# First-layer convolution taps tied behind score maxima, low weight parts formed by accumulating DMAs, probabilities transposed in row halves

## Chip, cores and metric

The kernel runs on one core of a Trainium2 chip. The metric is the device time of one execution in microseconds (us); the figure for a kernel is the median over its runs. Engines are named as the profile names them: PE is the matrix engine (PEld its weight loads), DVE the vector engine, ACT the scalar engine, POOL the GpSimd engine, SP the engine whose queue issues the loads.

## What is computed

Two layers over 256 latent tokens and 256 context tokens, width 1024. The first sub-layer of each layer has one input projection whose columns feed a convolution branch, an attention and two gates; the second is a gated MLP. Cut to the first sub-layer:

```python
h = modulate(rmsnorm(x, norm1_g[l]), sh1, sc1)
p = h @ w_in[l]                                   # GLU 1024 | q,k,v 3*512 | gates 2*1024
u = a * sigmoid(g)                                # a, g: the two halves of the GLU columns
u = dwconv1d(u, dw, dw_b)                         # 31 taps per channel, 512 channels
u = silu(layernorm(u, ln_g, ln_b));  y_conv = u @ w_conv_out
q, k = rope(q), rope(k)
y_attn = softmax(q k^T + window bias, all context keys) v @ w_na_out
x = x + g1 * ((sigmoid(gc) * y_conv + sigmoid(ga) * y_attn) @ w_out)
...
x = x + g2 * conv_ffn(modulate(rmsnorm(x, norm2_g[l]), sh2, sc2))
```

The context stream goes through the same weights in the first layer only; in the second layer it gives keys and values alone.

## The kernel before

**Weights.** All weights arrive as units of 128 x 1024 float32 (512 KB), in the order in which they are used, through four `raw` buffers that SP fills. `wunit` (L170, work in `wparts`, L150 to L168) splits a unit in two parts: ACT casts it to `whi` (L160, float32r), DVE subtracts to get `wlo = raw - whi` (L161). Four `whi` and four `wlo` buffers rotate. Every product is three matmuls (`mm3`, L178 to L181): `whi` with the high part of the activations, `whi` with the low part, `wlo` with the high part. `unit8` (L193) returns the eight 128-column blocks of a unit. A first-layer unit over both streams (512 columns) is 24 matmuls.

**Units of the input projection.** `U_IN` to `U_IN + 29` are the six remaining GLU units, four q, four k and sixteen gate units. In the first layer the order is q and k of pair 0, two GLU units, q and k of pair 1, two GLU units and so on (`qk`, L749; `glu_groups`, L617), then gates (`gate`, L624).

**Convolution.** `glu` (L602) writes a padded tile `u`; each of the 31 taps is one DVE instruction over 512 columns (L589, L591) that accumulates in `cb`. In the first layer there are two `u` tiles for four channel blocks. Taps wait in a list and are emitted by `conv_run` (L595), `rate[0]` of them (2 in the first layer, 3 in the second) at each `slot()`. A slot comes twice in a 512-column group (L183 to L191) and gives each side generator one step.

**Attention.** `Attention.step` (L416) is a side generator too. With `products` (L442) it issues the scores of two heads (one pair of head halves on rows 0 to 63 and 64 to 127 of the array, L440), with `scores` (L451) the maxima on DVE (L458), exponentials (L461) and normalization (L464) on ACT; `ctx_scores` (L468 to L484) does it for context queries. A later step calls `turn` (L486), which transposes the probabilities (16 PE transposes of 128 x 128: L494 for latent and L499 for context queries) through four PSUM banks, and copies each bank to a `pT` tile on ACT (L495, L500). The step after that calls `values` (L504), whose matmuls (L512) need `pT`. There are four latent and two context steps in the first layer, four latent steps in the second.

**Layer norm of the convolution.** `layer_norm` (L832) emits the taps that are left, adds the four `cb` blocks (two adds on POOL, L842 and L843, one on DVE, L844), and sums over channels on PE (L847).

**Order.** Instructions stand on each engine in the order in which the builder places them; within an engine they start in order. `tc.issue_after(x)` keeps what is issued under it behind instruction `x` in that order.

Of the kernel before, what the change touches and what calls it, by code (L numbers as in the profile page):

```python
# [45 lines left out]
def trunk(ctx: ExitStack, tc: tile.TileContext, xt, cvec, crow, wall, wada, params, bias_t, rope_t, out):  # L46
# [136 lines left out]
    def group(ps, ws, xh, xl, c):  # L183
# [201 lines left out]
    class Attention:  # L385

        def __init__(self, l, eb, T, V, oh, ol):
            self.l, self.eb, self.T, self.V, self.oh, self.ol = l, eb, T, V, oh, ol  # L390
            self.todo, self.soft, self.pv, self.n, self.at = [], [], [], 0, 0
            self.ctx, self.pairs, self.last = [], 0, None

# [22 lines left out]
        def step(self, now=False):  # L416
            self.n += 1
            since = self.n - self.at
            if not now and (since < (4 if self.todo else 3 if self.soft else 2) or not self.todo and self.pairs < 4):
                return  # L420
            if self.todo and not now and self.n - self.todo[0][0] < 2:
                return
            self.at = self.n
            pv, self.pv = self.pv, []
            soft, self.soft = self.soft, []
            for what, its, pps in soft:
                with tc.issue_after(self.last.ins), tc.issue_after(self.done.ins):
# [3 lines left out]
            if self.todo:  # L431
                _, what, its = self.todo.pop(0)
                outs = [self.products(it, [psum(t) for t in tags]) for it, tags in zip(its, (("sc", "sc"), ("pt", "main")))]
                self.soft.append((what, its, [(self.scores if what == LAT else self.ctx_scores)(it, o) for it, o in zip(its, outs)]))

# [15 lines left out]
        def scores(self, it, out):  # L451
            qt, bt = it[1], it[-1]
            pps = []
            for i, ps in enumerate(out):

                mx = small([P, 1], "mx")
                p2, b2 = ps.rearrange("p (a k) -> p a k", a=2), bt[:, 2 * qt + i :: 4 - 2 * qt - i, :]
                dve.tensor_tensor_reduce(p2, p2, b2, -1.0, 3.0e38, ALU.add, ALU.min, mx)  # L458
                pp = self.eb.tile([P, 512], F32, tag="pp", bufs=4, name=nm("pp"))
                sm = small([P, 1], "sm")  # L460
                self.exp = act.activation(pp, ps, AF.Exp, bias=mx, scale=-1.0, accum_out=sm)  # L461
                ri = small([P, 1], "ri")
                dve.reciprocal(ri, sm)
                self.done = act.mul(pp, pp, ri)  # L464
                pps.append(pp)
            return pps

        def ctx_scores(self, it, out):  # L468
            pps = []
            for ps in out:  # L470
                mx = small([P, 2], "mx2")
                dve.tensor_reduce(mx, ps.rearrange("p (q k) -> p q k", q=2), AX.X, ALU.max, negate=True)
                pp = self.eb.tile([P, 512], F32, tag="pp", bufs=4, name=nm("pp"))
# [12 lines left out]
        def turn(self, what, its, pps):  # L486

            pts = [self.eb.tile([P, 4, S], F32, tag="pT", bufs=4, name=nm("pT")) for _ in range(2)]
            for n, tags in enumerate((("sc", "sc"), ("pt", "main"))):
                for i, pp in enumerate(pps[n]):  # L490
                    pt = psum(tags[i])
                    if what == LAT:
                        for kt in range(4):
                            pe.transpose(sl(pt, kt), sl(pp, kt), ident)  # L494
                        act.copy(pts[i][:, :, n * P : (n + 1) * P], pt.rearrange("p (k q) -> p k q", k=4))  # L495
                    else:
                        for t in range(2):
                            for kt in range(2):
                                pe.transpose(pt[:, kt * S + t * P : kt * S + (t + 1) * P], sl(pp, 2 * t + kt), ident)  # L499
                        act.copy(pts[i][:, 2 * n : 2 * n + 2, :], pt.rearrange("p (k q) -> p k q", k=2))  # L500
            js = [its[0][0]] if what == LAT else [it[0] for it in its]
            self.pv.append((what, js, pts))

        def values(self, what, js, pts, bank):  # L504
            po = psum(bank)
            kts = range(4) if what == LAT else range(2, 4)
            for n, j in enumerate(js):
                c = slice(n * S, (n + 1) * S)
                for kt in kts:
                    for i in range(2):  # L510
                        h = 2 * j + i
                        pe.matmul(  # L512
                            po[i * HD : (i + 1) * HD, c], self.V[kt][:, h * HD : (h + 1) * HD],
                            pts[i][:, 2 * n + kt - kts[0], :], start=kt == kts[0], stop=kt == kts[-1],
                        )
# [42 lines left out]
    for l in range(DEPTH):  # L558
# [5 lines left out]
        with ExitStack() if last else start as e1a:  # L564
# [17 lines left out]

            taps = []

            def conv_tap(j, t):
                w = par[:, l * NPAR + DW + j * TAPS + t : l * NPAR + DW + j * TAPS + t + 1]
                src = us[j % NU_][:, :, t : t + S]
                if t == 0:
                    dve.tensor_scalar(cb[j], src, w, pr(l, DWB + j, 1), ALU.mult, ALU.add)  # L589
                else:  # L590
                    dve.scalar_tensor_tensor(cb[j], src, w, cb[j], ALU.mult, ALU.add)  # L591

            rate = [0]

            def conv_run():  # L595
                while True:
                    for _ in range(rate[0]):
                        if taps:
                            conv_tap(*taps.pop(0))
# [33 lines left out]
            with ExitStack() as e1b:  # L633
                eb = e1b.enter_context(tc.tile_pool(name=f"eb{l}", bufs=1))
                V = [eb.tile([P, CONV], F32, name=f"V{l}_{t}") for t in range(4)]
                att = Attention(l, eb, T, V, oh, ol)

# [107 lines left out]
                conv = conv_run()  # L745
                rate[0] = 3 if last else 2
                add_side(conv)
# [68 lines left out]
            with ExitStack() as e1c:  # L816
# [15 lines left out]
                def layer_norm():  # L832
# [392 lines left out]
```

## Time and profile before

| | us |
|---|---|
| three runs | 1127.99, 1128.18, 1128.67 (median 1128.18) |
| the profiled execution | 1127.64 |
| its span, first to last instruction | 1125.9 |
| PE busy | 1114.1 |
| DVE busy | 908.3 |
| ACT busy | 563.6 |
| POOL busy | 14.7 |

A row of the profile names the source line, engine, operation and tiles as `output<-inputs`; of a matmul the moving operand stands first and the stationary one second. `64*128 64x256` says 64 rows of the array, 128 columns, and a moving operand of 64 x 256. Durations of matmuls overlap, since they are pipelined, so the time that one takes from PE is read from the distance between starts.

### The profile page before, as it was taken

What the parts mean: (1) busy time and instruction counts of PE and PEld (TensorE: products, weight loads), DVE (VectorE), ACT (ScalarE), POOL (GpSimd) and SP (SyncE); (2) the same over time, 40 slices, a digit from 0 to 9 for tenths busy, and PEclk for the clock granted to TensorE, in tenths of its full rate; (3) what the DMA queues carried; (4) which work ended last, traced back from release to release, by engine and by line L of the source; (5) the groups of instructions that cost most, each with busy time, mean ns of one, the idle gap of its engine ahead of it and who ended that gap; (6) DMA issues with size and microseconds to landing.
All of it is one profiled execution on the core that took longest, in us unless ns stands there. A gap on an engine that the chain in (4) does not pass through costs nothing.

```text
span 1125.9 us, 17731 instructions
## 1 busy us (share of the span) xinstructions
PE 1114.1 (99%) x6828; PEld 963.0 (86%) x6828; DVE 908.3 (81%) x1631; ACT 563.6 (50%) x934; POOL 14.7 (1%) x24
## 2 busy tenths in 40 slices
PE   9999999999999999999999999999999999999997
PEld 7778777787789988888888888989888999999997
DVE  5689999685778788888898555789996898988773
ACT  4347657542333543434343222544677667766642
POOL 0000000000000000000000000000000000000000
PEclk9999999999999999999999999999999999999999
DMA  9833231536734354554556665556433575565781
GB/s 364 282 94 103 75 118 38 206 97 214 245 118 138 114 161 150 168 169 149 168 171 215 219 191 186 180 181 187 145 126 121 167 250 163 188 194 181 219 268 58
DMA packets 53941, 190.83 MB, mean 169 GB/s; under 512 B 6240, under 2 KB 6496, under 8 KB 53856
## 3 DMA queue, kind: packets, MB, share of 16 engines
q1 hardware_dynamic: 53568, 189.65, 52.1%
q8 instruction: 54, 0.88, 0.3%
q14 instruction: 31, 0.25, 0.1%
q10 hardware_dynamic: 288, 0.04, 0.0%
HBM read 188.62 MB, written 1.05 MB: 168 GB/s over the span
## 4 chain that ended last, share of the span: by engine, by line
PE 83%; DVE 9%; issue 6%; ACT 2%; DMA 0%; POOL 0%; POOLq 0%; DVEq 0%; SPq 0%; ACTq 0%
PE main L179 24%; PE main L181 24%; PE main L180 24%; DVE cb L591 4%; PE main L644 4%; DVE wlo L161 1%; PE sc L181 1%; PE sc L179 1%; PE sc L180 1%; PE po L202 1%; PE po L512 1%; PE sc L129 1%; PE sc L440 0%; DMA sb<-in_crow 0%; PE sc L494 0%
## 5 line engine op out<-in xcount | busy, mean ns | idle before, releaser
L179 PE MATMUL main<-h,whi 128*128 128x256 f32 (+1 forms) x1328 | 446.7, 337 | 0.0
L181 PE MATMUL main<-h,wlo 128*128 128x256 f32 (+1 forms) x1328 | 442.9, 335 | 1.0 <-DVE wlo L161 1.0
L180 PE MATMUL main<-h,whi 128*128 128x256 f32 (+1 forms) x1328 | 442.2, 334 | 0.1
L160 ACT CAST whi<-raw 128x1024 fp32r<-128x1024 f32 (+1 forms) x244 | 252.3, 1039 | 285.5 <-PE main L180 131.5
L161 DVE TENSOR_TENSOR wlo<-raw,whi 128x1024 fp32r<-128x1024 f32 (+1 forms) x244 | 292.9, 1207 | 112.5 <-ACT whi L160 108.0
L179 PEld LDWEIGHTS main<-h,whi 128*128 128x128 f32 x1328 | 249.4, 188 | 32.1 <-issue 3.6
L181 PEld LDWEIGHTS main<-h,wlo 128*128 128x128 f32 x1328 | 249.3, 188 | 29.6 <-DVE wlo L161 1.5
L180 PEld LDWEIGHTS main<-h,whi 128*128 128x128 f32 x1328 | 249.8, 188 | 28.5 <-DVE h L367 0.5
L591 DVE SCALAR_TENSOR_TENSOR cb<-u,par,cb 128x512 f32<-128x512 f32 (+1 forms) x240 | 140.4, 609 | 1.4
L271 DVE CUSTOM_DVE_ANT_0 t<-raw,sb,par 128x1024 bf16<-128x1024 f32 x100 | 126.7, 1277 | 1.0 <-ACT sb L255 0.7
L179 PE MATMUL main<-fh,whi 128*128 128x256 f32 (+1 forms) x386 | 123.0, 319 | 0.0
L180 PE MATMUL main<-fl,whi 128*128 128x256 f32 (+1 forms) x386 | 122.9, 319 | 0.0
L181 PE MATMUL main<-fh,wlo 128*128 128x256 f32 (+1 forms) x386 | 122.9, 318 | 0.0
L180 PEld LDWEIGHTS main<-fl,whi 128*128 128x128 f32 x386 | 72.7, 188 | 5.6
L179 PEld LDWEIGHTS main<-fh,whi 128*128 128x128 f32 x386 | 72.7, 188 | 5.6
L181 PEld LDWEIGHTS main<-fh,wlo 128*128 128x128 f32 x386 | 72.7, 188 | 5.5
L963 ACT ACTIVATE t<-main,par 128x512 f32<-128x512 f32 (+1 forms) x82 | 50.6, 667 | 39.0 <-PE main L181 39.0
L964 DVE SCALAR_TENSOR_TENSOR t<-main,par,t 128x510 f32<-128x510 f32 (+1 forms) x82 | 47.5, 615 | 10.2 <-ACT t L963 9.8
L967 DVE SCALAR_TENSOR_TENSOR t<-main,par,t 128x510 f32<-128x510 f32 (+1 forms) x82 | 46.6, 609 | 0.0
L366 ACT ACTIVATE h<-t,mod 128x256 fp32r<-128x256 f32 x56 | 25.4, 502 | 36.1 <-DVE t L365 36.1
L898 DVE SCALAR_TENSOR_TENSOR x<-main,mod,x 128x256 f32<-128x256 f32 x48 | 22.1, 479 | 23.5 <-PE main L181 23.3
L644 PE MATMUL main<-whi,h 128*128 128x512 f32 x128 | 40.6, 402 | 0.1
(221 smaller groups left out, 1188.2 us busy)
## 6 DMA issues: line engine op xcount, KB each, us to landing
raw<-in_wall SPq DMA_DIRECT2D x239, 512.0 KB, 4.2
raw<-in_wada SPq DMA_DIRECT2D x88, 512.0 KB, 4.3
bias<-in_bias_t SPq DMA_DIRECT2D x8, 640.0 KB, 4.8
row<-in_wada SPq DMA_DIRECT2D x8, 512.0 KB, 4.7
sb<-in_crow SPq DMA_DIRECT2D x5, 512.0 KB, 6.0
x<-in_xt SPq DMA_DIRECT2D x8, 256.0 KB, 4.4
raw<-in_wall SPq DMA_DIRECT2D x8, 256.0 KB, 7.1
out<-t SPq DMA_DIRECT2D x3, 256.0 KB, 2.1
```

The costliest lines, as they stand in the source:

```text
L160: act.copy(hi[:, c], r[:, c])
L161: dve.tensor_tensor(lo[:, c], r[:, c], hi[:, c].bitcast(F32), ALU.subtract)
L179: pe.matmul(ps, w[0], xh, start=start, stop=False)
L180: pe.matmul(ps, w[0], xl, start=False, stop=False)
L181: pe.matmul(ps, w[1], xh, start=False, stop=stop)
L271: dve.tensor_tensor_reduce(tmp().bitcast(BF16), r, v, 1.0, pr(l, BADA + n, 1), ALU.mult, ALU.add, mods[l][:, n, s : s + 1])
L366: high = act.activation(hi[:, c], y[:, c], AF.Identity, bias=b)
L591: dve.scalar_tensor_tensor(cb[j], src, w, cb[j], ALU.mult, ALU.add)
L644: mm = pe.matmul(pv[t], h1[n == 1][k][:, c], w[n == 2][:, b], start=k + n == 0, stop=k == KD - 1 and n == 2)
L963: act.activation(c, pv_, AF.Identity, bias=pr(l, FDB + t, 1), scale=w[1])
L964: dve.scalar_tensor_tensor(c[:, :, 1:], pv_[:, :, : S - 1], w[0], c[:, :, 1:], ALU.mult, ALU.add)
L967: dve.scalar_tensor_tensor(c[:, :, : S - 1], pv_[:, :, 1:], w[2], c[:, :, : S - 1], ALU.mult, ALU.add)
```

## The change

What it does, part by part:

1. **Low parts by adding transfers.** For the 30 units from `U_IN` of the first layer, `wadded` replaces `wunit`: ACT casts to `whi` as before and then writes `wlo = -whi` (L200); a DMA that POOL issues adds `raw` onto `wlo` (L201). DVE's subtraction is gone for these units, and the `raw` buffer is free once that DMA has read it.
2. **Turning on the row halves.** `turn` issues each 128 x 128 transpose as two: rows 0 to 63 and rows 64 to 127 of the probabilities, each with 128 stationary columns and 64 moving columns, into two different PSUM banks. One tile `pT` holds both heads. This holds in both layers.
3. **Steps.** A turn that has no values to go with it is a step of its own; the scores follow one slot later (`alone`, `late`).
4. **Taps tied.** In the first layer each tap is kept behind the last score maximum issued so far (`after`); the rate goes from 2 to 2.5 a slot, and there are four `u` tiles in place of two.
5. **Layer norm sums.** In the first layer the two POOL adds move to DVE.
6. The scratch for software-generated DMA descriptors is set to 1024.

```diff
+ADDED = {(0, u) for u in range(U_IN, U_IN + 30)}
...
+    def wadded(l, u):
+        r = raw_unit(wall[l, u])
+        hi = wp.tile([P, UW], F32R, tag="whi", bufs=4, name=nm("whi"))
+        lo = wp.tile([P, UW], F32R, tag="wlo", bufs=4, name=nm("wlo"))
+        act.copy(hi, r)
+        act.mul(lo, hi.bitcast(F32), -1.0)
+        pool.dma_start(lo, r, accum_op=ALU.add)
+        return hi, lo
...
     def unit8(l, u, at=None):
-        w = wunit(l, u, at)
+        w = wadded(l, u) if (l, u) in ADDED else wunit(l, u, at)
...
             since = self.n - self.at
-            if not now and (since < (4 if self.todo else 3 if self.soft else 2) or not self.todo and self.pairs < 4):
+            alone = self.soft and not self.pv and not self.late
+            if not now and since < (4 if self.todo or alone else 3 if self.soft else 2) and not self.late:
                 return
-            if self.todo and not now and self.n - self.todo[0][0] < 2:
+            if not now and not alone and not self.todo and self.pairs < 4:
                 return
+            if not now and not alone and self.todo and self.n - self.todo[0][0] < 2:
+                return
+            if self.late:
+                self.late, self.at = False, self.n
+                return self.issue()
+            if alone and not now:
+                self.late = True
...
-                dve.tensor_tensor_reduce(p2, p2, b2, -1.0, 3.0e38, ALU.add, ALU.min, mx)
+                self.after[0] = dve.tensor_tensor_reduce(p2, p2, b2, -1.0, 3.0e38, ALU.add, ALU.min, mx)
...
         def turn(self, what, its, pps):
-            pts = [self.eb.tile([P, 4, S], F32, tag="pT", bufs=4, name=nm("pT")) for _ in range(2)]
+            pT = self.eb.tile([P, 2, 4, S], F32, tag="pT", bufs=2, name=nm("pT"))
             for n, tags in enumerate((("sc", "sc"), ("pt", "main"))):
+                outs = [psum(t).rearrange("p (i s q) -> p i s q", i=2, s=4) for t in tags]
                 for i, pp in enumerate(pps[n]):
-                    pt = psum(tags[i])
+                    for s in range(4):
+                        src = s if what == LAT else s % 2 * 2 + s // 2
+                        for pt, r in zip(outs, HALF):
+                            pe.transpose(pt[:, i, s], sl(pp, src)[r], ident[r, r])
+                for pt, r in zip(outs, HALF):
                     if what == LAT:
-                        for kt in range(4):
-                            pe.transpose(sl(pt, kt), sl(pp, kt), ident)
-                        act.copy(pts[i][:, :, n * P : (n + 1) * P], pt.rearrange("p (k q) -> p k q", k=4))
+                        act.copy(pT[:, :, :, n * P + r.start : n * P + r.stop], pt)
...
-            NU_ = KC if last else 2
+            NU_ = KC
...
             def conv_tap(j, t):
+                if after[0] is not None and not last:
+                    with tc.issue_after(after[0].ins):
+                        tap(j, t)
+                else:
+                    tap(j, t)
...
-                rate[0] = 3 if last else 2
+                rate[0] = 3 if last else 2.5
...
-                    pool.tensor_tensor(sm[:, :T], flat[0], flat[1], ALU.add)
-                    pool.tensor_tensor(sm[:, :T], sm[:, :T], flat[2], ALU.add)
+                    eng = pool if last else dve
+                    eng.tensor_tensor(sm[:, :T], flat[0], flat[1], ALU.add)
+                    eng.tensor_tensor(sm[:, :T], sm[:, :T], flat[2], ALU.add)
...
-    nc = bacc.Bacc("TRN2", target_bir_lowering=False, num_devices=1)
+    nc = bacc.Bacc("TRN2", target_bir_lowering=False, num_devices=1, dynamic_dma_scratch_size=1024)
```

How it stands on the engines. On PE, the second turn of the first layer before the change; `pp` is a probability tile, `sc`, `pt` and `main` are PSUM banks:

```order
L494 MATMUL sc_1009<-ident,pp_845 128x128 x4
L494 MATMUL sc_1015<-ident,pp_853 128x128 x4
L494 MATMUL pt_1021<-ident,pp_861 128x128 x4
L494 MATMUL main_1027<-ident,pp_869 128x128 x4
L440 MATMUL sc_1033<-qk_967,qk_921 128x512
```

The same turn with the change (rows that alternate in the same way are left out):

```order
L518 MATMUL sc_978<-ident,pp_857 128x64
L518 MATMUL sc_979<-ident,pp_857 128x64
...
L518 MATMUL sc_978<-ident,pp_865 128x64
L518 MATMUL sc_979<-ident,pp_865 128x64
...
L518 MATMUL pt_998<-ident,pp_873 128x64
L518 MATMUL main_999<-ident,pp_873 128x64
...
L518 MATMUL pt_998<-ident,pp_881 128x64
L518 MATMUL main_999<-ident,pp_881 128x64
```

Sixteen transposes became sixteen pairs, the two of a pair on different row halves and into different banks; the scores (L440, now L463) no longer follow at once but after one more group of 24 matmuls, since this first turn is a step of its own.

On ACT, the stretch between that turn's copies and the next softmax, before:

```order
L768 ACTIVATE qk_967<-t_961 128x256
L160 CAST whi_1320<-raw_1319 128x1024
L495 COPY pT_1007<-sc_1009 128x4x128
L495 COPY pT_1008<-sc_1015 128x4x128
L495 COPY pT_1007<-pt_1021 128x4x128
L495 COPY pT_1008<-main_1027 128x4x128
L461 ACTIVATE pp_1051,sm_1052<-sc_1033,mx_1049 128x512
```

And with the change:

```order
L199 CAST whi_1327<-raw_1325 128x1024
L200 ACTIVATE wlo_1328<-whi_1327 128x1024
L521 COPY pT_977<-sc_978 128x8x64
L521 COPY pT_977<-sc_979 128x8x64
L521 COPY pT_977<-pt_998 128x8x64
L521 COPY pT_977<-main_999 128x8x64
L803 ACTIVATE qk_1024<-main_940 128x256
L803 ACTIVATE qk_1024<-t_1018 128x256
L199 CAST whi_1375<-raw_1373 128x1024
L200 ACTIVATE wlo_1376<-whi_1375 128x1024
L484 ACTIVATE pp_1084,sm_1085<-sc_1066,mx_1082 128x512
```

Each cast is followed by a second pass that writes the negated high part (`wlo`), ahead of the exponentials.

On DVE, the second set of score maxima (`mx`), before:

```order
L161 TENSOR_TENSOR wlo_1228<-raw_1226,whi_1227 128x1024
...
L591 SCALAR_TENSOR_TENSOR cb_1_199<-u_1_212,par,cb_1_199 128x512
L591 SCALAR_TENSOR_TENSOR cb_0_198<-u_0_211,par,cb_0_198 128x512
L458 ISA sc_1033,mx_1049<-sc_1033,bias_878 128x512
L458 ISA sc_1034,mx_1057<-sc_1034,bias_878 128x512
L591 SCALAR_TENSOR_TENSOR cb_0_198<-u_0_211,par,cb_0_198 128x512
L463 RECIPROCAL ri_1054<-sm_1052 128x1
L458 ISA pt_1041,mx_1065<-pt_1041,bias_878 128x512
```

And with the change:

```order
L623 SCALAR_TENSOR_TENSOR cb_1_199<-u_1_212,par,cb_1_199 128x512
L481 ISA sc_1066,mx_1082<-sc_1066,bias_890 128x512
L481 ISA sc_1067,mx_1090<-sc_1067,bias_890 128x512
L486 RECIPROCAL ri_1087<-sm_1085 128x1
L481 ISA pt_1074,mx_1098<-pt_1074,bias_890 128x512
L486 RECIPROCAL ri_1095<-sm_1093 128x1
L481 ISA main_1075,mx_1106<-main_1075,bias_890 128x512
L623 SCALAR_TENSOR_TENSOR cb_1_199<-u_1_212,par,cb_1_199 128x512 x2
```

No low part stands ahead of the maxima any more, and no tap between them.

More of the change, by code (lines that the diff above doesn't have):

```diff
@@ L385, in trunk, with __init__ @@
     class Attention:
-        def __init__(self, l, eb, T, V, oh, ol):
+        def __init__(self, l, eb, T, V, oh, ol, after):
+            self.after = after
             self.l, self.eb, self.T, self.V, self.oh, self.ol = l, eb, T, V, oh, ol
             self.todo, self.soft, self.pv, self.n, self.at = [], [], [], 0, 0
-            self.ctx, self.pairs, self.last = [], 0, None
+            self.ctx, self.pairs, self.last, self.late = [], 0, None, False
         def pair(self, j, q, k, bt, last):
@@ L430, in step, with issue @@
                 self.values(*work, "sc" if work[0] == CTX and not (soft or self.todo) else "po")
[L431 to L434, printed above, removed]
+            if self.todo and not self.late:
+                self.issue()
+        def issue(self):
+            _, what, its = self.todo.pop(0)
+            outs = [self.products(it, [psum(t) for t in tags]) for it, tags in zip(its, (("sc", "sc"), ("pt", "main")))]
+            self.soft.append((what, its, [(self.scores if what == LAT else self.ctx_scores)(it, o) for it, o in zip(its, outs)]))
         def product(self, out, q, k, c, d):
@@ L591, in conv_tap @@
                     dve.scalar_tensor_tensor(cb[j], src, w, cb[j], ALU.mult, ALU.add)
-            rate = [0]
+            rate = [0.0]
             def conv_run():
+                due = 0.0
                 while True:
-                    for _ in range(rate[0]):
+                    due += rate[0]
+                    while due >= 1:
+                        due -= 1
                         if taps:
```

18 lines of the change are left out of this document (9 added, 9 removed).

## Prediction

> **What bounds the kernel.** I read the page's head first: busy times, the chain that ended last by engine, and the table of what PE waited for.
>
> ```profile
> span 1125.9 us, 17731 instructions
> PE 1114.1 (99%) x6828; PEld 963.0 (86%) x6828; DVE 908.3 (81%) x1631; ACT 563.6 (50%) x934; POOL 14.7 (1%) x24
> PE 83%; DVE 9%; issue 6%; ACT 2%; DMA 0%; POOL 0%; POOLq 0%; DVEq 0%; SPq 0%; ACTq 0%
> PE main L181 <- DVE wlo L161: 1.0, 2, 0.6
> PE pt L228 <- ACT t L221: 0.6, 1, 0.6
> PE po L351 <- POOL rs L346: 0.4, 1, 0.4
> ```
>
> PE is busy 99% of the span, and the rows of its waits are 1.0 us and less. The two waits for `wlo` stand at 903 and 963 us, behind the 30 units in question. So a gain must come from PE having less to do. The stretches where the change acts are seen in the table by window (sum, then PE, PEld, DVE, ACT, POOL busy, clock, DMA share, GB/s): the first layer's attention, the gates behind it, and the second layer's attention.
>
> ```profile
> 104.00:199.00 95.00, 95.00 (x539) 74.28 (x536) 94.46 (x184) 68.33 (x146) 2.99 (x2) 1.00 0.27 81
> 199.00:250.00 51.00, 50.42 (x234) 39.75 (x233) 38.72 (x58) 24.55 (x36) 1.99 (x1) 1.00 0.50 165
> 768.00:870.00 102.00, 102.00 (x761) 91.23 (x759) 94.03 (x223) 68.77 (x133) 1.60 (x2) 1.00 0.44 137
> ```
>
> From 104 to 199 us DVE is full (94.46 of 95) and yet PE never stops (95.00 of 95): taps are a stock that DVE works off in the gaps, and PE does not wait for it. Taking work from DVE there is worth at most the 0.58 us that PE lacks between 199 and 250 us. The clock is 1.00 throughout, so nothing is to be had there.
>
> **Part 1: the transposes.** The turns are the one thing on PE that gets smaller.
>
> ```profile
> L494 PE MATMUL sc<-ident,pp x64: 270/273/276, 100.7 to 856.2; 128*128 128x128 f32 x64
> L499 PE MATMUL sc<-ident,pp x16: 272/272/273, 132.4 to 191.2; 128*128 128x128 f32 x16
> ...
> 109.98 1.04 PE L494 MATMUL sc<-ident,pp 128*128 128x128 f32 x8
> 110.86 0.60 PE L494 MATMUL pt<-ident,pp 128*128 128x128 f32 x4
> 111.29 0.38 PE L494 MATMUL main<-ident,pp 128*128 128x128 f32 x2
> ```
>
> The `sc` banks take half of a turn's transposes, so there are 2 x (64 + 16) = 160, ten turns of 16. In a turn eight start between 109.98 and 110.86 and four more by 111.29: 0.88 / 8 = 0.110 and 0.43 / 4 = 0.108, say 0.109 us each, 160 x 0.109 = 17.4 us in all. What sets the 0.109, the streaming of 128 columns or the load of the next stationary block? The loads of other widths tell.
>
> ```profile
> L512 PEld LDWEIGHTS po<-pT,V 128*64 128x64 f32 x144 | 9.5, 136 | 5.4 <-issue 1.3
> L494 PEld LDWEIGHTS sc<-ident,pp 128*128 128x128 f32 x64 | 7.4, 141 | 0.8
> L440 PEld LDWEIGHTS main<-qk,qk 64*128 64x128 f32 x36 | 6.0, 185 | 0.2
> L336 PEld LDWEIGHTS pt<-one,ss 128*128 128x128 f32 x32 | 4.2, 190 | 0.4 <-DVE ss L322 0.3
> L202 PEld LDWEIGHTS po<-raw,sil 128*32 128x32 f32 x128 | 3.2, 109 | 4.0 <-issue 2.2 <-ACT whi L680 0.4
> ```
>
> 32, 64 and 128 columns take 109, 136 and 190 ns: 0.84 ns a column above a fixed 82 ns, which I take to be latency that overlaps. The transposes' loads, at 141, look like 59 ns of real loading; an ordinary 128-column load like 104 to 108. So I take the 0.109 for streaming, at two passes per column. Halving the moving operand to 64 columns gives 0.055. Whether the two halves of a pair run beside each other is shown by the scores, which already use the row halves:
>
> ```profile
> 114.75 0.28 PE L440 MATMUL main<-qk,qk 64*128 64x256 f32 x1
> 114.75 0.28 PE L440 MATMUL pt<-qk,qk 64*128 64x256 f32 x1
> 114.87 0.28 PE L440 MATMUL main<-qk,qk 64*128 64x256 f32 x1
> 114.87 0.28 PE L440 MATMUL pt<-qk,qk 64*128 64x256 f32 x1
> ...
> 233.59 0.95 PE L336 MATMUL pt<-one,ss 128*128 128x1 f32 x8
> 234.40 0.47 PE L179 MATMUL main<-h,whi 128*128 128x512 f32 x1
> ```
>
> Two of them start together every 0.12 us, though each has a load of 185 ns (104 net): two loads in 0.12 us are beside each other. A pair of half transposes is therefore bounded from below by its stream, 0.055, and from above by two loads one after the other, 2 x 0.059 = 0.118; if the half's load takes the ordinary 104 ns, beside each other, a pair takes 0.104, and the eight L336 matmuls with one moving column, 0.81 / 8 = 0.101 apart, show such a bound by loads alone. I take 0.062, load and a little issue, being nearest to the pairs of L440 run beside each other with the transposes' own load: 160 x 0.062 = 9.9 us, a change of **-7.5** (ends: 160 x 0.055 = 8.8, -8.6; 160 x 0.118 = 18.9, +1.5).
>
> [...]
>
> **Part 2: going in and out of the row halves.** At 104 us PE leaves the half-row scores:
>
> ```profile
> 103.98 0.39 PE L440 MATMUL main<-qk,qk 64*128 64x512 f32 x1
> 104.30 0.50 PE L179 MATMUL main<-h,whi 128*128 128x512 f32 x1
> 104.64 0.39 PE L180 MATMUL main<-h,whi 128*128 128x512 f32 x1
> 104.87 0.40 PE L181 MATMUL main<-h,wlo 128*128 128x512 f32 x1
> ```
>
> The starts lie 0.32, 0.34 and 0.23 us apart where 0.23 is the step without a switch: 0.09 + 0.11 = 0.20 us for one switch. [...] A turn now begins with such a switch where it used to continue whole-array work; what follows a turn (values in column halves or scores in row halves) had its own switch before. Eight turns get one more, 8 x 0.2 = 1.6; the first turn of each layer, now a step of its own, gets an entry and an exit and the scores behind it theirs, some 0.5 each: 1.0. [...]
>
> **Part 3: low parts, taps, layer norm.** DVE gives up 30 subtractions, ACT gets 30 passes.
>
> ```profile
> L591 DVE SCALAR_TENSOR_TENSOR cb<-u,par,cb 128x512 f32<-128x512 f32 x120 | 86.3, 739 | 0.7
> L161 DVE TENSOR_TENSOR wlo<-raw,whi 128x1024 fp32r<-128x1024 f32 x26 | 31.6, 1215 | 11.7 <-ACT whi L160 8.2 <-PE sc L181 3.2 <-PE sc L440 0.3
> L160 ACT CAST whi<-raw 128x1024 fp32r<-128x1024 f32 x27 | 28.2, 1050 | 30.5 <-PE main L180 27.7 <-issue 2.7
> ```
>
> DVE: 30 x 1.215 = 36 us less, and two layer norm additions more, at about a tap's 0.74 each. With 36 us of room the rate of 2.5 taps and the order behind the maxima cost it nothing that PE sees; without that room the taps would be left over for the layer norm. Its relief is worth to PE the one wait in that stretch, 0.6, partly: **-0.5** (ends 0 and -1.0, this wait and that for `rs`). The four `u` tiles are cleared early on POOL, which has 14.7 us of work. ACT: 30 x 1.05 = 31.5 us more between 60 and 250 us; in 95 us it was busy 68.33, and gets about half of the 30, 16 us: 84 of 95, full enough to make things late. What stands behind a second pass in its queue is the exponentials, the copies of `pT` and the rotations. A turn now also needs both probability tiles of a bank before it is done, and in the second layer the last of them come just before it is due:
>
> ```profile
> 854.29 1.37 ACT L464 ACTIVATE pp<-pp,ri 128x512 f32<-128x512 f32 x2
> 855.47 1.04 PE L494 MATMUL sc<-ident,pp 128*128 128x128 f32 x8
> ```
>
> The normalization ends at 855.66, when the old turn had begun with the other tiles. I price lateness at 0.1 us for each of ten turns, **+1.0** (ends 0 and 0.3 each, +3.0).
>
> The adding transfer does not occur in the trace. What it may take is read from the slack: the tightest unit is the one cast at 211.22.
>
> ```profile
> 211.22 1.05 ACT L160 CAST whi<-raw 128x1024 fp32r<-128x1024 f32 x1
> 223.68 0.40 PE L179 MATMUL main<-h,whi 128*128 128x512 f32 x1
> ...
> raw<-in_wall SPq DMA_DIRECT2D x239, 512.0 KB, 4.2
> raw<-in_wall SPq DMA_DIRECT2D x8, 256.0 KB, 7.1
> ```
>
> Its first product is at 223.68 and the low part is needed 0.46 later; from 211.22 that is 12.9, less two passes of 1.05: 10.8 us for POOL's issue and the transfer. Other units have more. Loads of the same size land after 4.2 us, the slowest row is 7.1; since the sum must be read, added and written back I put it at twice the first, 8.4, and so inside the slack: nothing. The `raw` buffer comes back after 4.2 + 1.05 + 1.05 + 8.4 = 14.7 us, inside four units of 24 x 0.232 = 5.57 us. If the cover goes, PE waits: at 14.2 us (twice 7.1) 3.4 us for the tightest unit, and several such units make +4 to +12. DMA queues are idle enough here (share 0.27 and 0.50); POOL's queue holds one `rs` instruction among the transfers, behind which two units' issue may wait.
>
> **Sum.** -7.5 + 2.6 - 0.5 + 1.0 = -4.4. The profiled execution took 1127.64, so 1123.2 by its measure; it lies 0.54 under the median of 1128.18, so I predict **1123.8 us**. With the ends near to the values taken (pairs 0.055 to 0.07, switches 1.6 to 3.2, lateness 0 to 2) it is 1120 to 1126.
>
> **Rivals.**
> 1. *A pair is no faster than a whole transpose* (slower). The half's load takes 104 ns as every other 128-column load does, or two halves load in turn at 59. Place: the ten turns. Then the first term is 0 to +1.5 (taken 0.5), the switches of 2.6 and the lateness stay: +0.5 + 2.6 + 0.5 (lateness less relief) = +3.6, 1131.8. It decides from where 160 x (0.109 - t) is below 3.1 us, a pair of 0.090 us. For it: L336's 0.101 and its 190 ns; against it the 141 ns of the transposes' loads and the start of two L440 together. [...]
> 2. *The adding transfers come late.* From 10.8 us on the tightest unit waits, then the neighbours through the buffer ring. At 14.2 us each, +4 to +12 on the forecast less what it wins: 1128 to 1136, middle 1132. For it: no row has such a transfer, and POOL must issue it in order. Against it: 4.2 us for a plain one and a DMA share of 0.27.
> 3. *The change is swallowed.* The pair gains half (0.08 us, -4.6), and ACT's 84 of 95 us makes softmax late by 0.3 a turn: -4.6 + 2.6 - 0.5 + 3.0 = +0.5, 1128.7; with one of the two alone about 1126. That the DVE relief does nothing for the time, which the change seems to be after, is already in the forecast.
>
> **How the numbers follow.** Chances: forecast 0.57, first rival 0.18, second 0.12, third 0.13. About 0.2% (2.3 us) is what a measurement of this kernel can tell from no change; the forecast lies 4.4 below, and its range to 1126 is faster almost throughout: faster 0.57. The third is within: 0.13. The first and second are above 1130.4 in the main: slower 0.30. The range reaches from 1119.5, the forecast with pairs at their stream and no lateness, to 1133, which takes in the first rival and the lower half of the second; left out are the worst of the second and little else.
>
> **What the changed profile would show.** The pairs of half transposes starting 0.055 to 0.07 us apart, two at the same start and a turn of 16 pairs in about 1.0 us in place of 1.75, would bear out the first term; 0.10 or more the first rival. PE's start distances at a turn's entry of 0.2 us over the step bear out the second. In the table of PE's waits, a row of `L181` for POOL's transfer or `wlo` would be the second rival, and a row of a turn for ACT's `pp` the third. DVE should fall by about 35 us, ACT rise by 31, with PE still at 99%. The prediction is wrong if a transposed half streams or loads as long as a whole, or if a low part takes over 11 us to arrive.

## The result, and the profile after

The change makes the kernel slower: 1140.04 us (median of 4 runs, 1138.39 to 1141.94) against 1128.09 in runs beside it, a ratio of 1.0106 with a 95% interval of 1.0088 to 1.0124. The forecast was 1123.8, and 1119.5 to 1133 at its ends.

The page's head of the kernel after, its chain by engine, and three of PE's waits that are new or longer than before:

```profile
span 1139.0 us, 18150 instructions
PE 1115.2 (98%) x6988; PEld 957.9 (84%) x6988; DVE 879.8 (77%) x1603; ACT 592.9 (52%) x965; POOL 38.0 (3%) x54
PE 77%; DVE 10%; DMA 6%; ACT 5%; issue 2%; SPq 0%; DVEq 0%; POOLq 0%; ACTq 0%
PE main L182 <- DMA wlo<-raw: 5.2, 3, 2.2
PE po L362 <- POOL rs L357: 2.0, 1, 2.0
PE sc L463 <- ACT pT L521: 1.4, 2, 1.1
```

DMA, at 0% of the chain before, now has 6% of it. I matched the low-part products of both profiles in order (there are 1932 in each) and compared their starts. After is 1.7 us ahead when the gates begin (197.68 against 199.40), 11.4 behind at 283 us, stays there to the second layer's attention, and ends 13.3 behind. So the first layer's attention gains, the gates lose 13 us, the second layer's attention loses 2. The gates in the table by window (same columns as before), of before and then of after:

```profile
199.00:272.00 73.00, 72.42 (x341) 56.92 (x340) 51.91 (x80) 29.44 (x43) 1.99 (x1) 1.00 0.54 177
```

```profile
199.00:283.00 84.00, 74.72 (x332) 57.14 (x331) 51.48 (x84) 35.33 (x48) 8.07 (x9) 0.96 0.71 203
```

PE was idle 0.6 us there and now is idle 9.3; and the granted clock is 0.96 (see the last section). DVE has 0.4 us less to do, so its relief lies elsewhere. Why PE stops is read one engine further back. SP's queue, which issues the loads, from 60 to 285 us; first of before (units by L157, modulation rows by L147), then of after:

```profile
SPq L157 <- DVE wlo L161: 96.8, 21, 11.5
SPq L147 <- DVE wlo L161: 31.8, 7, 17.6
```

```profile
SPq L148 <- DMA wlo<-raw: 161.7, 27, 9.9
```

A load waits until its `raw` buffer is free. That was in the main DVE's subtraction, 128.6 us in 28 waits; now it is the landing of the adding transfer, 161.7 us in 27. The queue does not wait longer in all (212 us before, 208 after, all rows together): a load finds the buffers taken in both kernels. What differs is how late it then is for its cast. One buffer's turn in the profile of after, on SP, ACT and POOL:

```profile
230.87 0.33 SPq L148 DMA_DIRECT2D raw<-in_wall  x1
...
241.31 0.33 SPq L148 DMA_DIRECT2D raw<-in_wall  x1
241.73 0.38 SPq L148 DMA_DIRECT2D raw<-in_wada  x1
```

```profile
234.27 1.05 ACT L199 CAST whi<-raw 128x1024 fp32r<-128x1024 f32 x1 [5.73 <-DMA raw<-in_wall]
235.35 1.06 ACT L200 ACTIVATE wlo<-whi 128x1024 fp32r<-128x1024 f32 x1
```

```profile
236.82 0.88 POOL L201 DMA_DIRECT2D wlo<-raw  x1 [9.58 <-ACT wlo L200]
237.38 1.38 POOL L357 TENSOR_TENSOR rs<-red,mhalf 128x4 f32<-128x4 f32 x1
```

Load issued at 230.87, landed and cast at 234.27, negated by 236.41, transfer issued at 236.82, buffer loaded again at 241.31: 10.4 us, of which the last 4.5 are the transfer. The buffer comes free when the transfer has landed (241.25). The next load in SP's queue, a modulation row (`in_wada`, from which DVE forms the modulation of this layer's second sub-layer), waits behind it and goes at 241.73, though DVE was done with its buffer at 234.40. These rows come through the same four buffers: between 199 and 262 us there are 8 loads from `in_wall` and 8 from `in_wada`.

And a row stays long: those loaded at 205.03, 213.24 and 221.92 us are read by DVE until 231.23, 234.40 and 248.61. While rows hold three of the four buffers, the units go through the fourth one after the other (loads at 219.41, 230.87 and 241.31). Rows stay as long in before (210.77 to 234.40, 220.40 to 246.39), so little is spare there too: between 201 and 242 us a unit's load goes every 6.1 us in before and every 9.4 in after, and a unit is 5.57 us of products.

The cast's idle time says who is ahead: before, its longest part was waiting for PE to give back a `whi` buffer (27.7 us, ACT ahead of PE); now it waits for loads:

```profile
L199 ACT CAST whi<-raw 128x1024 fp32r<-128x1024 f32 x27 | 28.4, 1051 | 40.4 <-DMA raw<-in_wall 25.9 <-PE main L181 14.5
wlo<-raw POOLq DMA_DIRECT2D x30, 512.0 KB, 5.5
```

Load by load it is plainer. In the gates (199 to 262 us) of before a unit's load has landed 0.9 us ahead of its cast (median of 9); in after 0.02 us, seven of eight casts start as the load lands. Between 60 and 199 us the loads are 15.7 and 11.3 us ahead, and there nothing is lost.

The transfers themselves land in 5.5 us (median, 4.4 to 9.8), better than the 8.4 of the forecast.

The halved turn is as forecast. The second turn, of after (the listing ahead of the prediction that is called the second turn shows the first, at 100.7 us in before, behind which the scores follow at once; behind this one come values):

```profile
110.17 0.71 PE L518 MATMUL sc<-ident,pp 64*128 64x64 f32 x16
...
111.09 0.22 PE L518 MATMUL pt<-ident,pp 64*128 64x64 f32 x1
111.09 0.22 PE L518 MATMUL main<-ident,pp 64*128 64x64 f32 x1
111.15 0.22 PE L518 MATMUL pt<-ident,pp 64*128 64x64 f32 x1
111.15 0.22 PE L518 MATMUL main<-ident,pp 64*128 64x64 f32 x1
111.31 0.65 PE L536 MATMUL po<-pT,V 128*64 128x256 f32 x4
```

Two start together every 0.06 us, and the turn takes 1.14 us to the values (before: 109.98 to 111.82, 1.84). With the 0.10 us more ahead of it (328 ns in place of 229 from the last product to the first transpose) a turn gains 0.60, ten gain 6.0.

### The profile page after: what moved, and what is told of

It is laid out like the page before. It is cut to its first block, busy times and chain, and to the rows that moved or that the text cites. A ratio compares the mean times of both kernels' runs of the same rounds, so it can differ in the third digit from the quotient of the medians.

```text
span 1139.0 us, 18150 instructions
## 1 busy us (share of the span) xinstructions
PE 1115.2 (98%) x6988; PEld 957.9 (84%) x6988; DVE 879.8 (77%) x1603; ACT 592.9 (52%) x965; POOL 38.0 (3%) x54
## 4 chain that ended last, share of the span: by engine, by line
PE 77%; DVE 10%; DMA 6%; ACT 5%; issue 2%; SPq 0%; DVEq 0%; POOLq 0%; ACTq 0%
PE main L180 23%; PE main L182 23%; PE main L181 23%; DVE cb L623 3%; DVE wlo L162 3%; DMA wlo<-raw 3%; DMA raw<-in_wall 3%; PE main L679 2%; PE po L536 1%; PE sc L180 1%; PE sc L182 1%; PE sc L181 1%; PE po L213 1%; ACT whi L161 1%; DMA x<-in_xt 1%
## 5 line engine op out<-in xcount | busy, mean ns | idle before, releaser
L161 ACT CAST whi<-raw 128x1024 fp32r<-128x1024 f32 (+1 forms) x214 | 220.8, 1037 | 263.9 <-DMA raw<-in_wall 140.5
L162 DVE TENSOR_TENSOR wlo<-raw,whi 128x1024 fp32r<-128x1024 f32 (+1 forms) x214 | 256.6, 1207 | 108.7 <-ACT whi L161 107.3
L199 ACT CAST whi<-raw 128x1024 fp32r<-128x1024 f32 x30 | 31.5, 1051 | 41.3 <-DMA raw<-in_wall 26.7
```

The source lines that it names most:

```text
L161: act.copy(hi[:, c], r[:, c])
L162: dve.tensor_tensor(lo[:, c], r[:, c], hi[:, c].bitcast(F32), ALU.subtract)
L199: act.copy(hi, r)
```

## Experiments

Ratios are to the kernel before in runs on the same chip (its medians there: 1127.6 to 1128.1), with 95% intervals. A difference of less than some 1.4 us between two of these runs lies within their intervals.

### Is it the adding transfers, and what of them?

**After, without the adding transfers.**

```diff
-ADDED = {(0, u) for u in range(U_IN, U_IN + 30)}
+ADDED = set()
```

> The kernel after with the low parts of the 30 units formed on VectorE again (no adding transfer, no second ACT pass); all other parts stay. Theory A (the adding transfers keep the raw buffers longer, and SP's loads behind them come late): the loss between 199 and 283 us goes, so about 13 us less than after's 1140: 1127, 1124 to 1130. Rival C (taps tied to the maxima, layer norm sums on VectorE or the lone steps make the loss): stays at 1137 or more. Rival B (only PE's wait for late low parts, 5.2 us in the table of waits): about 1135.

Measured: 1129.66, 1.0021 (1.0012 to 1.0030). 10.4 of the 12 us are gone; as A has it. What is left of the change is no gain but 2 us of loss, which A does not explain.

**Before, with the adding transfers only** (`wadded` and the scratch size, nothing else).

> The kernel before with nothing but the adding transfers for the 30 units (and the descriptor scratch of the change). A: 1128 plus about 12 = 1140, 1136 to 1144, with SP's raw loads behind the transfers' landing. B: PE's waits for the low parts alone, 1133. C: 1127 to 1129, VectorE's relief being worth nothing.

Measured: 1140.08, 1.0108 (1.0093 to 1.0123). Part 1 alone makes as large a loss. In this profile PE does not wait for an adding transfer by name at all:

```profile
PE po L362 <- POOL rs L357: 4.0, 1, 4.0
PE main L510 <- ACT pp L493: 2.4, 1, 2.4
```

The stop for `rs` stands behind a late load: the cast whose transfer POOL issues just ahead of `rs` had waited 7.28 us for its load. The stop for probabilities at 196.6 us does not: ACT had waited 2.94 us for maxima on DVE. Product by product this run is 5.7 us further behind before at 200 us than at 60 us, and loses 6.6 more by 245 us. So not all of its loss lies where that of after does, and that both come to 12 us is in part chance.

**Before, buffers held for nothing.**

```diff
+        act.copy(hi, r)
+        dve.tensor_tensor(lo, r, hi.bitcast(F32), ALU.subtract)
+        act.mul(sp_, hi.bitcast(F32), -1.0)
+        pool.dma_start(sp_, r, accum_op=ALU.add)    # sp_: a spare tile, three buffers
```

> The kernel before, with the low parts still formed on VectorE, and beside that the same ACT pass and the same adding transfer for the 30 units, into a spare tile that nobody reads. It tells the hold of the raw buffer from the lateness of the low part: no product waits for a transfer here. A (raw buffers held, loads late): as slow as with the adding transfers in use, 1138 to 1145. B (late low parts): 1128 to 1131.

Measured: 1138.53, 1.0098 (1.0084 to 1.0112). No product needs these transfers, and the time is almost that of the real ones. SP's and PE's waits in its profile:

```profile
SPq L148 <- DMA spare<-raw: 132.8, 26, 11.1
```

```profile
PE pt L348 <- DVE ss L334: 7.9, 1, 7.9
```

Here all of the loss lies in the gates (1.1 us behind before at 200 us, 11.8 at 240), at the stop shown and the lower clock behind it. So late low parts (rival B) are not the mechanism; the hold is, together with ACT's pass, which this run has too. The next run keeps both the pass and the transfers.

**After, six raw buffers.**

```diff
-        r = wp.tile([P, UW], F32, tag="raw", bufs=4, name=nm("raw"))
+        r = wp.tile([P, UW], F32, tag="raw", bufs=6, name=nm("raw"))     # in all three places
```

> The kernel after with six raw buffers in place of four. A: two more loads are under way, the stalls of 199 to 283 us go: 1125 to 1129. B: the transfers last as long as before, low parts late as before: 1135 or more. C: no change, 1140.

Measured: 1129.53, 1.0019 (1.0010 to 1.0028), 10.5 us less than after. The same ACT passes and transfers, two more buffers: the loss is gone, and so it was the buffers. It lies just above the range that A gave, and 2 us above before like the run without transfers. SP's queue and ACT's casts:

```profile
SPq L148 <- DMA wlo<-raw: 147.0, 26, 10.1
```

```profile
L199 ACT CAST whi<-raw 128x1024 fp32r<-128x1024 f32 x27 | 28.3, 1049 | 27.6 <-PE main L181 20.0 <-DMA raw<-in_wall 7.6
```

The queue waits for the transfers almost as long as with four buffers, and it costs nothing, since the loads lie further ahead: in the gates a unit's load goes every 6.3 us and lands 0.9 us ahead of its cast, much as in before. Nor is it that loads land more slowly beside the transfers: between 199 and 262 us a unit's load takes 3.7 us in before, 4.3 in after and 5.0 here.

**Before, six raw buffers** and the smaller descriptor scratch (part 6), nothing else.

> The kernel before with six raw buffers and nothing else (and the smaller descriptor scratch that makes room for them). PE does not wait for raw loads there, so A expects no change: 1127 to 1128.5. If more loads under way are worth time by themselves: 1126.5 or less.

Measured: 1127.79, 1.0000 (0.9992 to 1.0009): no change. More buffers are worth nothing here by themselves, and the scratch costs nothing.

**After, 24 units added, four buffers.**

> The kernel after, four raw buffers, adding transfers for the first 24 units only. A, with the place that the alignment shows (the loss of 13 us lies between 199 and 283 us, where the second layer's ada rows share the ring with the last units): 1129 to 1132. If the hold costs in all units alike: about 1137.

Measured: 1135.73, 1.0064 (1.0050 to 1.0078): a miss. I had put the loss on the last six units; they make 4.3 us of it, and 6.1 against the run without transfers remain (the rows that share the buffers there are the first layer's, not the second's). The profile shows how a late load reaches PE in this run; ACT:

```profile
229.73 1.05 ACT L161 CAST whi<-raw 128x1024 fp32r<-128x1024 f32 x1 [4.37 <-DMA raw<-in_wall]
...
231.21 1.66 ACT L329 ACTIVATE t<-cb 128x512 f32<-128x512 f32 x3
```

```profile
PE pt L347 <- DVE ss L333: 4.1, 1, 4.1
```

A unit cast in the ordinary way waits 4.4 us for its load, since the ring is still late from the added ones; the squares for the layer norm (L329) stand behind that cast in ACT's queue, DVE's sums behind the squares, PE behind the sums. Here the late load does its harm through the queue in which its cast stands.

### Where do the 6 us of the halved turns go?

**Before, halved turns only.**

> The kernel before with nothing but the halved transposes (turn and values of the change; the steps as before, a turn followed at once by scores). A turn takes 1.14 us in place of 1.84 in the profile of after, with 0.1 us more ahead of it: ten turns give -6.0. Theory D (the lone steps, not the halves, are what the second layer loses): 1122 to 1124. Rival E (the halves finish before ACT's copies, and the scores wait for the banks): 1126 or more.

Measured: 1129.19, 1.0011 (1.0002 to 1.0020). D fails, E holds: the halves alone gain nothing. The second turn shows where it goes. PE and ACT of before, then of this run:

```profile
111.82 1.95 PE L512 MATMUL po<-pT,V 128*64 128x256 f32 x16
113.70 1.09 PE L440 MATMUL sc<-qk,qk 64*128 64x256 f32 x11
```

```profile
112.31 0.60 ACT L606 ACTIVATE t<-main 128x512 f32<-128x512 f32 x1
112.81 1.07 ACT L495 COPY pT<-sc 128x512 f32<-128x512 f32 x2
```

```profile
111.71 1.95 PE L513 MATMUL po<-pT,V 128*64 128x256 f32 x16
114.50 0.87 PE L440 MATMUL sc<-qk,qk 64*128 64x256 f32 x3 [0.84 <-ACT pT L498]
```

```profile
113.37 0.60 ACT L607 ACTIVATE t<-main 128x512 f32<-128x512 f32 x1
113.87 1.07 ACT L498 COPY pT<-sc 128x512 f32<-128x512 f32 x2
```

The scores write the `sc` banks that ACT must first copy to `pT`. Before, the first copy was under way since 112.81 and the scores began at 113.70: PE arrived when ACT was done, by a few tenths. This run is 0.5 us behind before when its first turn begins; counted from there PE reaches the values 0.6 us earlier and ACT its first copy 0.6 us later, and PE waits 0.84 us. ACT is later because the maxima ahead of it are. DVE ahead of the first of them, before and then here:

```profile
100.61 3.39 DVE L591 SCALAR_TENSOR_TENSOR cb<-u,par,cb 128x512 f32<-128x512 f32 x5
```

```profile
101.10 4.05 DVE L592 SCALAR_TENSOR_TENSOR cb<-u,par,cb 128x512 f32<-128x512 f32 x6
```

The order of instructions came out with one tap more there, 0.66 us, so half of this wait is not the shorter turn's doing. ACT was busy half of the span (50% in before), and yet in this stretch it is a chain with no slack behind PE. A second place in this run is the last turn for context queries, where PE stops 1.13 us for probabilities (`PE pt L495 <- ACT pp L482`). Behind that stop the granted clock falls:

```profile
192.00:196.00 4.00, 3.84 (x26) 2.27 (x28) 3.82 (x6) 3.97 (x8) 0.00 (x0) 0.57 0.00 0
```

The sixteen values matmuls take 3.21 us there, where the same take 1.95 at 111.71. This part of the run's loss is the clock's.

**After with six buffers, steps as before** (no lone turn).

> The kernel after with six raw buffers and the steps as before (no lone turn). D: against 1129.5 with the lone steps it gains the 2.0 us that the second layer lost in its alignment, and the 1 us of switches: 1125 to 1127, the second layer then ahead of before. E: 1129 or more.

Measured: 1128.42, 1.0004 (0.9995 to 1.0013), 1.1 us less than with lone turns by the medians and 1.7 by the ratios, between what D and E gave. In the alignment the second layer's attention now loses nothing in place of 2.0; D's place is right. But the first layer is 1.2 us worse without them, and so less is won than D had.

**After without adding, lone turns in the first layer only.**

```diff
-            alone = self.soft and not self.pv and not self.late
+            alone = self.l == 0 and self.soft and not self.pv and not self.late
```

> The kernel after without adding transfers and with lone turns in the first layer only. D (lone steps in the second layer lose 2 us there): against 1129.7 with them 1127 to 1128.5. If not: 1129.5.

Measured: 1127.90, 1.0004 (0.9995 to 1.0013), 1.8 less than with lone turns in both layers: as D says. In the second layer the lone turn moves the copies to `pT` in ACT's order behind rotations (L803) that wait for DVE. ACT in the run without adding and with lone turns in both layers:

```profile
827.80 0.39 ACT L803 ACTIVATE qk<-main 128x256 fp32r<-128x256 f32 x1 [1.69 <-DVE t L798]
829.10 0.42 ACT L803 ACTIVATE qk<-t 128x256 fp32r<-128x256 f32 x1 [0.92 <-DVE t L800]
...
830.62 1.07 ACT L521 COPY pT<-sc 128x512 f32<-128x512 f32 x2
```

```profile
831.26 0.50 PE L463 MATMUL sc<-qk,qk 64*128 64x512 f32 x1 [1.02 <-ACT pT L521]
```

The turn was over at 828.3, and the copies begin 2.3 us later.

**Six buffers, copies split between ACT and DVE** (of a turn's two banks one by `dve.tensor_copy`), with 30 units and with 24.

> Six raw buffers, steps as before, adding transfers for 30 units, and of each two banks of a turn one copied by VectorE in place of ScalarE. E (the shorter turn is given back because the next scores wait for ScalarE's copies of the banks): against 1128.4 without the split, the waits of scores for copies (1.3 us in the table, some 2.5 with the restarts) go: 1125 to 1127. If the copies aren't what holds: 1128 or more.

> Both edits together, the version to which the runs so far point: 1124.5 to 1126.5 where both theories hold, against before's 1127.9.

Measured: 1133.65, 1.0045 (1.0031 to 1.0058), and 1131.77, 1.0037 (1.0024 to 1.0049). Both miss: slower by 5. Taken at its word, the expectation counts this against E; but DVE's copies came later than ACT's, so the runs don't test it. Of the first run:

```profile
PE pt L347 <- DVE ss L333: 4.8, 1, 4.8
PE sc L452 <- DVE pT L510: 2.8, 3, 1.4
```

The scores now wait for DVE's copies longer than they did for ACT's (2.8 against 1.3), and PE stops 4.8 us for the layer norm's sums on DVE. That this is the work which DVE put off for the copies is likely and not shown.

**Six buffers, 24 units, whole transposes again**, against the same with halves (`six_raw_24_added`, below).

> As the version with six raw buffers, 24 added units and steps as before (1126.55), with whole transposes again. E (the time that halved turns save is given back to waits for the copies and the probabilities): 1126 to 1128, about the same. If the halves keep their 6 us: 1131 or more.

Measured: 1127.26, 0.9994 (0.9985 to 1.0002), against 1126.55 with halves. The halves are worth 0.7 us of their 6.0 by the medians, which the intervals don't tell from nothing. PE's waits between 60 and 985 us, with halves and with whole transposes:

```profile
PE sc L452 <- ACT pT L510: 1.3, 3, 0.8
PE main L182 <- DVE wlo L162: 1.0, 2, 0.5
PE po L525 <- DVE ol L532: 0.7, 1, 0.7
```

```profile
PE main L182 <- DVE wlo L162: 1.0, 2, 0.6
```

With whole transposes there is no wait in the attention at all. The waits of the attention listed are 2.0 us; each stop also costs some tenths beside what is listed (in after, around the stop of 1.68 us that ends at 254.33, two steps of products take from 252.26 to 254.67, 2.41 us in place of 2 x 0.23: 0.27 more than the stop). Matched with before product by product, the halves gain 0.9 us between 60 and 199 us, where six turns should save 3.6, and 0.1 in the second layer's attention, where four should save 2.4; whole transposes gain nothing in either. So 5.0 of the 6.0 are given back there. The listed waits explain less than half of that; the rest was not taken apart.

### The other parts

**Six buffers, taps not tied to the maxima.**

> The kernel after with six raw buffers, taps not kept behind the maxima (rate 2.5 as in after). If the tie protects the maxima: 1130.5 or more, with turns waiting for probabilities. If VectorE has room enough without it: within 1 us of 1129.5.

Measured: 1135.76, 1.0073 (1.0058 to 1.0087), 6.2 us more than tied. At 2.5 taps a slot the tie is needed: turns wait for probabilities (`PE pt L518 <- ACT pp L505`, 1.8 us in two) and the layer norm's sums for DVE (2.4 us).

**Six buffers, layer norm sums on POOL.**

> The kernel after with six raw buffers, the two layer norm additions of the first layer on GpSimd again, among the adding transfers in its queue. If the additions on VectorE are late behind its taps and cause the stop of 2 us near 230 us: 1127 to 1128.5. If not: 1129.5, or some tenths more.

Measured: 1129.10, 1.0010 (1.0001 to 1.0019), no different from 1129.53. PE's stop for `rs` is still there (`PE po L362 <- POOL rs L357`, 1.9 us), so the sums on DVE do not cause it.

**Six buffers, 24 units added, steps as before.**

> Six raw buffers, steps as before, adding transfers for the first 24 units in place of 30. If the stop of 1.2 us near 235 us comes from GpSimd's queue, where the layer norm's root stands behind a transfer's issue: 1126.5 to 1127.5. If not: 1128.4 as with 30.

Measured: 1126.55, 0.9988 (0.9979 to 0.9997); 1.9 less than with 30. The stop for `rs` is gone. In the profile of after, `rs` starts at 237.38 on POOL, behind the transfer that POOL issued at 236.82 and for which it had waited 9.58 us: a small instruction kept back by an issue that waits in the same queue. What `rs` reads had been ready since 233.2; with 24 units `rs` starts 0.1 us behind it.

**Six buffers, 24 units, lone turns in the first layer only**: the version to which the runs point.

> Six raw buffers, adding transfers for 24 units, lone turns in the first layer only. The lone turn takes away the stop of 0.8 us at 102 us (scores behind ScalarE's copies), and the second layer keeps the steps that did not lose there: against 1126.55 without any lone turn 1125 to 1126. If lone turns are worth nothing in the first layer either: 1126.5 or more.

Measured: 1125.50, 0.9976 (0.9966 to 0.9986): faster than both kernels, by 2.4 us than before and 14.5 than after. Against the same without transfers (1127.90, with four buffers) the transfers with enough buffers are worth 2.4 us. Against no lone turns (1126.55) it is 1.1 us, too little to show what the lone turn alone is worth in the first layer.

## Why the prediction was wrong, point by point

1. **The failed step: adding transfers at nothing.** The forecast said that the `raw` buffer comes back after 14.7 us, "inside four units" of 5.57 us, "nothing". The duration was not the fault (5.5 us for the transfer where 8.4 was assumed, and 10.4 for a whole turn of the buffer). The fault was to count four buffers for the units and to read the slack behind the cast only (10.8 us for the low part). The modulation rows share the buffers, one for every unit in the gates, and keep them for 21 to 27 us; in SP's queue a load that waits holds up what stands behind it (the row of 241.73 us, 7 us after its buffer was free); and ahead of the cast the loads of before had 0.9 us to spare in the gates. Held longer, the buffers let a unit's load go every 9.4 us, for 5.57 us of products. Measured: +12 us alone in before, +10.4 in after, gone with six buffers. What the rows do is read from the trace; no run took them off the buffers.
2. **The second rival had the right part and the wrong path.** It expected PE to stop at the low parts from 10.8 us on. PE did so for 5.2 us; but with nobody reading the transfers' result the kernel was nearly as slow (1138.53). Its "neighbours through the buffer ring" was the nearest that the forecast came to the cause, and its sign, a low part that takes over 11 us, did not show: the slowest transfer took 9.8.
3. **Transposes and switches: right in size, not in worth.** -7.5 and +2.6 (the 1.6 and the 1.0 for switches) make -4.9; the turns got 6.0 shorter, with 0.06 us a pair where 0.062 was said. The first rival falls. Whether the stream (0.055) or the load (0.059) sets the 0.06 no run tells, so that 0.062 was so near is in part luck; the "two passes per column" of the forecast was its author's estimate and is not shown. Nor does a run show what the 0.20 us of a switch is made of; what the changed profile shows is 0.10 us more ahead of the second turn.
4. **Lateness of +1.0 was mis-sized.** In the version with 24 units 5.0 of the 6.0 us are given back, 2.0 of them in waits for ACT's copies and for the attention's results. The argument that PE is busy 99% and waits for nothing hid that ACT arrived together with it; where PE was made faster, ACT's finish was the next bound (PE waits 0.84 us for it in the second turn of the run with halved turns only). The third rival, "the change is swallowed", described this part, though a pair gained all and not half.
5. **Relief of DVE, -0.5:** with six buffers and 24 units the transfers bring 2.4 us (the tie is in both runs compared), more than the bounds of 0 to -1.0; with four nothing of it is seen.
6. **`rs` on POOL:** I had named the instruction and given it no price. Without the last six units' transfers the kernel gains 1.9 us, and the stop for `rs` (1.2 us in the run with 30 units and six buffers) is gone.
7. **The range.** Its lower end of 1119.5 does not follow from what is named for it: pairs at their stream and no lateness give 1123.8 - 1.1 - 1.0 = 1121.7.

Not settled: how the 6.1 us of the first 24 units with four buffers divide between them, and how much of the 10 us of hold is ACT's pass and how much the transfer, since both were always tried together.

## What to carry over

Before a buffer is held longer, list everything that shares its ring with how long each keeps its place, and read how far the loads land ahead of their first use: that lead (0.9 us in the gates before, 0.02 after) is where the slack shows. The wait of the queue that issues them is not (it was 212 us in before, 208 in after, and 202 with six buffers). A stage made shorter on the bounding engine gains only as far as the engine that feeds it has slack at that place (the turns here got 6.0 us shorter and brought 0.7), so follow that engine's chain in the stretch and not its share of the span. Where an instruction that waits for others is put on a queue, list what small work stands behind it (here `rs`, a stop of 2.0 us in after).

## What was not expected of the hardware

Behind some of PE's stops the granted clock itself fell. The table by window of the kernel after, around the stop of 1.96 us that ends at 238.81:

```profile
236.00:239.00 3.00, 1.04 (x6) 0.56 (x5) 0.00 (x0) 1.49 (x3) 1.94 (x2) 1.00 0.31 61
239.00:243.00 4.00, 4.00 (x14) 3.19 (x14) 3.27 (x5) 0.00 (x0) 0.00 (x0) 0.57 0.64 117
243.00:247.00 4.00, 4.00 (x19) 3.24 (x18) 0.34 (x1) 2.05 (x3) 0.00 (x0) 1.00 0.60 230
```

Products of 512 columns start 0.43 us apart in the second window and 0.23 in the third: about 1.5 us lost on top of the stop. It comes twice in after (behind this stop and one of 2.16 us at 267 us), some 3 of its 13 us; not at all in before or in after with six buffers. In the run that holds buffers for nothing the clock is 0.50 from 240 to 248 us, behind the stop of 7.9. A stop of 1.98 us in the run with split copies and 30 units (ending at 223.24 us) was not followed by it, and one of 1.13 us among transposes was, in the run with halved turns only. So it followed stops of 1.13, 1.96 and 2.16 us and did not follow one of 1.98: the length of a stop alone does not decide it.
